# The last feature block of the down-projection, cut by token blocks at the kernel's end

## The chip, the cores and the metric

The kernel runs on one core of one Trainium2 chip. The metric is the device time of one execution in microseconds (us). The engines have short names: PE is TensorE (PEld its weight loads), DVE VectorE, ACT ScalarE, POOL GpSimd, and SP is SyncE, which here only issues DMAs.

## The reference, cut to what matters

One trunk layer of a streaming encoder over 1024 prompt tokens and 32 sample tokens. Only its end is touched by the change, the second half of the feed-forward block and the final norm:

```python
x = x + gt2 * ((jax.nn.silu(g) * up) @ w_down)      # D_FF = 2816 -> D_MODEL = 1024
y = x * rsqrt(mean(x * x, axis=-1) + EPS) * g_final # for prompt and sample
```

## The kernel before

**Layout.** Activations lie with the features on the 128 partitions and the tokens along the free dimension: `x2[j]` (j from 0 to 7) holds 128 of the 1024 residual features for all 1056 tokens. The tokens are worked on in three thirds of 352. The final norm sums over features, so at the end each 128 x 128 piece of `x2[j]` is transposed on PE; the output rows leave with tokens on the partitions.

**Down-projection of the last third.** The loop at the end of the listing (L2228) makes, for tokens `cut` = 704 to 1056 and for one feature block j after the other, a product over 22 K tiles (`NF`; the hidden features in blocks of 128). A float32 product is made of three single passes (`PASSES`: high x high, low x high, high x low, in fp32r), each with a weight load of 128 columns of its own: 66 matmuls of 352 columns for each j. They add up in one PSUM bank, `acc`. The weights of a feature block come in three parts of 8, 8 and 6 K tiles (`chunks`); DMA brings a part into `wraw`, ACT and DVE split it into high and low tiles (`wsp`, four of them, L417 and L418), and `W.use` / `W.used` keep the order of these steps. `piece_of[k, 2]` are the split activations of the K tile. After the 66 matmuls DVE adds `gt2 * acc` to `x2[j]` (L2249, 320 prompt and 32 sample columns).

**The end.** While the loop runs, the first 704 tokens are normalised and stored beside it (`finish_some`, `Finish`). For the last third there is the class `End`: three token blocks (`cuts`) of 128, 128 and 96 tokens (the last is 64 prompt and 32 sample tokens). After the first eight K tiles of j = 7, `ahead` transposes features 0 to 6 of all three blocks on PE, squares and sums them on ACT, adds the sums on POOL and multiplies the first 512 features by `g_final` (`gB`) on DVE; the remaining 14 K tiles of j = 7 (42 matmuls) run after its transposes. After DVE's add, `last` transposes the three pieces of j = 7, squares them, and makes 1/sqrt on POOL; then per block ACT scales features 0 to 511, DVE scales features 512 to 1023, and each half row is stored by its own DMA, one issued from ACT's queue and one from SP's.

**What sets the order.** Each engine runs its instructions in the order in which the code issues them; semaphores between the engines are placed by the framework, from which tile is written and read by whom.

Of the kernel before, what the change touches and what calls it, by code (L numbers as in the profile page):

```python
# [17 lines left out]
P = 128  # L18
# [36 lines left out]
class Weights:  # L55
# [8 lines left out]
    def add(self, block):  # L64
        self.blocks.append(block)
# [74 lines left out]
def hybrid_stream_step(  # L140
# [2024 lines left out]
    class End:  # L2165
# [9 lines left out]

        def take(self, j0, j1, part):
            for i, (a, b) in enumerate(self.cuts):
                h, n = j0 // 4, b - a
                py = self.py[i][h]
                for j in range(j0, j1):  # L2180
                    pe.transpose(py[:n, (j - 4 * h) * P:(j - 4 * h + 1) * P], x2[j][:, a:b], ident)
                act.activation(self.ys[i][:n, j0 * P:j1 * P], py[:n, (j0 - 4 * h) * P:(j1 - 4 * h) * P], AF.Square,
                               scale=D ** -0.5, accum_out=self.st[:n, part, i:i + 1])

        def ahead(self):
            self.take(0, 4, 0)
            self.take(4, KD - 1, 1)
            st = self.st
            pool.tensor_tensor(st[:, 0], st[:, 0], st[:, 1], op=ALU.add)
            pool.tensor_scalar(st[:, 0], st[:, 0], 1.0, EPS, op0=ALU.mult, op1=ALU.add)  # L2190
            for y, py, (a, b) in zip(self.ys, self.py, self.cuts):
                dve.tensor_tensor(y[:b - a, :512], py[0][:b - a], gB[:b - a, :512], op=ALU.mult)

        def last(self):
            self.take(KD - 1, KD, 2)
            st = self.st
            for i in range(3):
                pool.tensor_tensor(st[:, 0, i:i + 1], st[:, 0, i:i + 1], st[:, 2, i:i + 1], op=ALU.add)
                pool.tensor_tensor(st[:, 3, i:i + 1], st[:, 0, i:i + 1], mhalf[:, 0:1], op=ALU.pow)
            for i, (y, py, (a, b)) in enumerate(zip(self.ys, self.py, self.cuts)):  # L2200
                n, r = b - a, st[:b - a, 3, i:i + 1]
                act.activation(y[:n, :512], y[:n, :512], AF.Copy, scale=r)
                dve.scalar_tensor_tensor(y[:n, 512:], py[1][:n], r, gB[:n, 512:], op0=ALU.mult, op1=ALU.mult)
                for eng, cs in ((act, slice(0, 512)), (sp, slice(512, D))):
                    for q, u, v in col_segments(a, b):
                        out = y_sample[0, u - S:v - S] if q else y_prompt[0, u:v]
                        eng.dma_start(out[:, cs], y[u - a:v - a, cs])

# [19 lines left out]
    for j in range(KD):  # L2228
        if j == KD - 1:
            side.drain(job)  # L2230
            end = End()
        acc = bank()
        for w, (k0, k1) in zip(w_d1[j], chunks):
            wt = W.use(w)
            for k in range(k0, k1):
                while steps and (min(k + 4, NF - 1), 2) not in piece_of:
                    steps.pop(0)[2]()
                for q, (u, v) in enumerate(PASSES):
                    pe.matmul(acc, wt[(k - k0) // 4][:, u, (k - k0) % 4], piece_of[k, 2][:, v],  # L2239
                              start=(k == 0 and q == 0), stop=(k == NF - 1 and q == 2))  # L2240
                if k % 2 == 1:
                    side.tick()
            W.used(w)
            if j == KD - 1 and k0 == 0:
                end.ahead()
        while steps:
            steps.pop(0)[2]()
        for c, a, b in col_segments(cut, T):
            dve.scalar_tensor_tensor(x2[j][:, a:b], acc[:, a - cut:b - cut], gt2[:, c, j:j + 1], x2[j][:, a:b],  # L2249
                                     op0=ALU.mult, op1=ALU.add)  # L2250
    end.last()
    close_sl()
# [35 lines left out]
```

## Time and profile before

| what | us |
|---|---|
| median of 3 runs | 1606.16 |
| the runs | 1605.96 to 1606.76 |
| the profiled execution, its own time | 1606.87 |
| its span, first to last instruction | 1604.8 |
| PE's last matmul of the projection ends at | 1595.2 |

The profiled execution lies 0.7 us over the median, and 2.07 us of its time lie around the span. All times of the trace below count from the start of the span. How to read the page: busy shares are of the whole span; matmuls overlap, and the ends of their records are modelled, so the pace of a row of matmuls is its whole length divided by their number and not the duration of one.

### The profile page before, as it was taken

The page shows a single profiled execution, that of the slowest core. Times are in us where ns is not written, and L with a number is a line of the kernel's source. Part 1 is how long each engine was busy: PE and PEld are TensorE (multiplying, and loading weights), DVE is VectorE, ACT ScalarE, POOL GpSimd, SP SyncE. Part 2 cuts the span into 40 slices and gives each one's busy share as a digit, 9 for nine tenths or more (in the row PEclk, how much of TensorE's full clock was granted, in tenths as well). Part 3 has the DMA queues.
Part 4 walks back from the last instruction along what each step waited for, and adds up shares of the span by engine and source line. Part 5 has one row for each costly group of instructions (what it writes and reads, how often), then busy time and mean ns, then how long its engine had stood idle before and what let it go on. Part 6 is the DMA issues. An engine that isn't in the chain of part 4 may idle for free.

```text
span 1604.8 us, 27381 instructions
## 1 busy us (share of the span) xinstructions
PE 1575.5 (98%) x10244; PEld 1554.0 (97%) x10244; DVE 1138.7 (71%) x2186; ACT 785.9 (49%) x1747; POOL 446.0 (28%) x477
## 2 busy tenths in 40 slices
PE   7999999999999999999999999999999999999997
PEld 6989999999999999999999999999999999999997
DVE  7766564646776855546654699988898986799754
ACT  3655463544455644444443655554544444545443
POOL 2344243434332411000012100565565650000001
PEclk9999999999999999999999999999999999999999
DMA  9823323232222232675353311313222227427453
GB/s 361 276 72 92 98 82 102 88 122 84 70 80 80 67 96 70 121 268 176 121 152 114 106 54 46 102 54 106 81 80 94 67 82 253 135 79 250 133 157 126
DMA packets 210414, 192.45 MB, mean 120 GB/s; under 512 B 10706, under 2 KB 180618, under 8 KB 209258
## 3 DMA queue, kind: packets, MB, share of 16 engines
q1 hardware_dynamic: 205386, 187.82, 37.4%
q10 hardware_dynamic: 4640, 2.82, 0.6%
q8 instruction: 81, 1.33, 0.4%
q14 instruction: 51, 0.42, 0.1%
q0 software_dynamic: 256, 0.06, 0.0%
HBM read 152.19 MB, written 41.63 MB: 121 GB/s over the span
## 4 chain that ended last, share of the span: by engine, by line
PE 88%; DVE 5%; DMA 3%; ACT 2%; issue 1%; SPq 0%; ACTq 0%; POOL 0%; DVEq 0%; POOLq 0%
PE mm L451 39%; PE psb L1836 18%; PE mm L1836 10%; PE mm L2239 3%; PE mm L900 3%; PE psb L2239 2%; PE psV L799 2%; PE psb L2082 2%; PE psS L741 1%; DMA s<-in_w_ada_dram 1%; PE psT L768 1%; PE mm L2082 1%; DMA wraw<-in_w_in_dram 1%; DMA t<-in_x_sample_dram 1%; DVE st L755 1%
## 5 line engine op out<-in xcount | busy, mean ns | idle before, releaser
L451 PE MATMUL mm<-s,wsp 128*128 128x352 f32 x4104 | 689.1, 324 | 0.0
L451 PEld LDWEIGHTS mm<-s,wsp 128*128 128x128 f32 x4104 | 656.8, 188 | 2.0 <-issue 0.4
L418 DVE TENSOR_TENSOR wsp<-wraw,wsp 128x512 fp32r<-128x512 f32 (+1 forms) x280 | 236.6, 861 | 119.2 <-ACT wsp L417 117.6
L1836 PE MATMUL psb<-s,wsp 128*128 128x352 f32 x1611 | 271.7, 322 | 1.5 <-DVE wsp L418 0.8
L417 ACT ACTIVATE wsp<-wraw 128x512 fp32r<-128x512 f32 x336 | 199.6, 617 | 138.8 <-PE psb L1836 40.8
L1836 PEld LDWEIGHTS psb<-s,wsp 128*128 128x128 f32 x1611 | 260.5, 188 | 2.1 <-DVE wsp L418 1.1
L1836 PE MATMUL mm<-s,wsp 128*128 128x352 f32 x933 | 159.3, 322 | 0.0
L1836 PEld LDWEIGHTS mm<-s,wsp 128*128 128x128 f32 x933 | 151.2, 188 | 0.5 <-DVE wsp L418 0.5
L761 POOL TENSOR_SCALAR st<-st,mx 128x640 f32<-128x640 f32 (+5 forms) x72 | 56.6, 785 | 184.2 <-DVE mx L760 169.9
L1223 DVE SCALAR_TENSOR_TENSOR t<-wa,cmix,t 128x512 f32<-128x512 f32 x112 | 88.7, 797 | 15.2 <-DMA wa<-in_w_ada_dram 14.9
L418 POOL TENSOR_TENSOR wsp<-wraw,wsp 128x512 fp32r<-128x512 f32 x56 | 75.8, 1375 | 49.1 <-ACT wsp L417 47.5
L756 ACT ACTIVATE st<-st,mx 128x640 f32<-128x640 f32 (+5 forms) x72 | 47.9, 666 | 71.3 <-DVE mx L755 70.0
L755 DVE CUSTOM_DVE_ANT_0 st<-psS,bias 128x640 f32<-128x640 f32 (+5 forms) x72 | 44.3, 616 | 46.1 <-PE psS L741 33.6
L1783 POOL TENSOR_TENSOR t<-t,sl 128x352 f32<-128x352 f32 x19 | 18.3, 962 | 185.3 <-ACT sl L1781 185.3
L775 ACT ACTIVATE pT<-psT 128x640 fp32r<-128x640 f32 (+3 forms) x80 | 38.7, 494 | 62.9 <-PE psT L768 48.0
L2151 POOL TENSOR_TENSOR fst<-fst 128x1 f32<-128x1 f32 (+1 forms) x6 | 1.2, 194 | 236.6 <-ACT t L2144 236.6
L780 DVE TENSOR_TENSOR pT<-psT,pT 128x640 fp32r<-128x640 f32 (+3 forms) x80 | 44.0, 558 | 22.7 <-ACT pT L775 22.5
L1446 POOL TENSOR_TENSOR wraw<-wraw,raw 128x512 f32<-128x512 f32 x33 | 55.8, 1703 | 0.9
L900 PE MATMUL mm<-s,s 128*128 128x264 f32 (+3 forms) x432 | 54.8, 283 | 0.0
L2239 PE MATMUL mm<-s,wsp 128*128 128x352 f32 x330 | 54.4, 324 | 0.0
L2239 PEld LDWEIGHTS mm<-s,wsp 128*128 128x128 f32 x330 | 53.1, 188 | 0.0
L1446 POOL TENSOR_TENSOR wraw<-wraw 128x512 f32<-128x512 f32 x22 | 32.6, 1482 | 71.4 <-DVE wsp L418 70.6
(392 smaller groups left out, 2543.0 us busy)
## 6 DMA issues: line engine op xcount, KB each, us to landing
wraw<-in_w_in_dram SPq DMA_DIRECT2D x38, 512.0 KB, 3.9
wraw<-in_w_gate_up_dram SPq DMA_DIRECT2D x33, 512.0 KB, 3.7
wa<-in_w_ada_dram SPq DMA_DIRECT2D x64, 256.0 KB, 3.2
wraw<-in_w_down_dram SPq DMA_DIRECT2D x32, 512.0 KB, 3.7
a_d<-t SPq DMA_DIRECT2D x22, 528.0 KB, 2.7
g_d<-t SPq DMA_DIRECT2D x16, 528.0 KB, 5.1
x<-xres SPq DMA_DIRECT2D x16, 528.0 KB, 6.5
t<-g_d SPq DMA_DIRECT2D x16, 528.0 KB, 5.0
```

Source lines behind the costliest of these rows:

```text
L417: act.activation(dst[:, 0], src, AF.Copy)
L418: eng.tensor_tensor(dst[:, 1], src, f(dst[:, 0]), op=ALU.subtract)
L451: pe.matmul(pt[:, :hi - lo], wt[(w0 + k) // 4][:, a, (w0 + k) % 4], xt[k][:, b, lo:hi], start=(k == 0 and q == 0), stop=(k == n - 1 and q ...
L755: dve.tensor_tensor_reduce(so, sv, bi, -1.0, 3.0e38, ALU.add, ALU.min, mx[:n, 1:2])
L756: act.activation(st[:n, :w], st[:n, :w], AF.Exp, bias=mx[:n, 1:2], scale=-1.0, accum_out=mx[:n, 2:3])
L761: pool.tensor_scalar(st[:n, :w], st[:n, :w], mx[:n, 3:4], 1.0, op0=ALU.mult, op1=ALU.mult)
L900: pe.matmul(pt[:n, :wd], hs[k][:, a, i * P:i * P + n], whl[b][:, k, :wd], start=(k == 0 and q == 0), stop=(k == KD - 1 and q == 2))
L1223: dve.scalar_tensor_tensor(ac[:, c], wa, cmix[:, c, k:k + 1], ac[:, c], op0=ALU.mult, op1=ALU.add)
L1446: self.eng.tensor_tensor(a(dst), a(x), a(y), op=op)
L1836: pe.matmul(acc, wt[:, a, k], x[k][:, b], start=(start and not onto and k == 0 and q == 0), stop=(stop and k == 3 and q == 2), skip_group_ ...
L2082: pe.matmul(acc, wt[k // 4][:, u, k % 4], piece_of[k, i][:, v], start=(k == 0 and q == 0), stop=(k == KP - 1 and q == 2))
L2239: pe.matmul(acc, wt[(k - k0) // 4][:, u, (k - k0) % 4], piece_of[k, 2][:, v], start=(k == 0 and q == 0), stop=(k == NF - 1 and q == 2))
```

## The change

The last 14 K tiles of feature block 7 are no longer multiplied with all 352 tokens at once. They run three times, with tokens 704 to 832, 832 to 960 and 960 to 1056, over the same weight tiles, into the matching columns of `acc`. `End.last` is split: `norm` (transpose, square, POOL's 1/sqrt) and `put` (the scalings and the stores) work on one block. The norm of a block stands behind the products of the next block, `put` of the first block behind the add of the third. A block's two halves leave in one DMA of whole rows: from SP's queue for prompt rows, from ACT's for the 32 sample rows. Both weight parts are split before `ahead`, no longer one before and one behind it.

```diff
-        def last(self):
-            self.take(KD - 1, KD, 2)
+        def norm(self, i):
+
+            self.take(i, KD - 1, KD, 2)
             st = self.st
-            for i in range(3):
-                pool.tensor_tensor(st[:, 0, i:i + 1], st[:, 0, i:i + 1], st[:, 2, i:i + 1], op=ALU.add)
-                pool.tensor_tensor(st[:, 3, i:i + 1], st[:, 0, i:i + 1], mhalf[:, 0:1], op=ALU.pow)
-            for i, (y, py, (a, b)) in enumerate(zip(self.ys, self.py, self.cuts)):
-                n, r = b - a, st[:b - a, 3, i:i + 1]
-                act.activation(y[:n, :512], y[:n, :512], AF.Copy, scale=r)
-                dve.scalar_tensor_tensor(y[:n, 512:], py[1][:n], r, gB[:n, 512:], op0=ALU.mult, op1=ALU.mult)
-                for eng, cs in ((act, slice(0, 512)), (sp, slice(512, D))):
-                    for q, u, v in col_segments(a, b):
-                        out = y_sample[0, u - S:v - S] if q else y_prompt[0, u:v]
-                        eng.dma_start(out[:, cs], y[u - a:v - a, cs])
+            pool.tensor_tensor(st[:, 0, i:i + 1], st[:, 0, i:i + 1], st[:, 2, i:i + 1], op=ALU.add)
+            pool.tensor_tensor(st[:, 3, i:i + 1], st[:, 0, i:i + 1], mhalf[:, 0:1], op=ALU.pow)
+
+        def put(self, i):
+            (a, b), y = self.cuts[i], self.ys[i]
+            n, r = b - a, self.st[:b - a, 3, i:i + 1]
+            act.activation(y[:n, :512], y[:n, :512], AF.Copy, scale=r)
+            dve.scalar_tensor_tensor(y[:n, 512:], self.py[i][1][:n], r, gB[:n, 512:], op0=ALU.mult, op1=ALU.mult)
+            for q, u, v in col_segments(a, b):
+                out = y_sample[0, u - S:v - S] if q else y_prompt[0, u:v]
+                (act if q else sp).dma_start(out, y[u - a:v - a])
...
+        def products(wt, k0, k, a, b):
+            for q, (u, v) in enumerate(PASSES):
+                pe.matmul(acc[:, a - cut:b - cut], wt[(k - k0) // 4][:, u, (k - k0) % 4],
+                          piece_of[k, 2][:, v, a - cut:b - cut], start=(k == 0 and q == 0),
+                          stop=(k == NF - 1 and q == 2), skip_group_check=j == KD - 1)
...
         for w, (k0, k1) in zip(w_d1[j], chunks):
+            if j == KD - 1 and k0:
+                continue
...
+    wts = [(W.use(w), *c) for w, c in zip(w_d1[-1][1:], chunks[1:])]
+    end.ahead()
+    for i, (a, b) in enumerate(end.cuts):
+        for wt, k0, k1 in wts:
+            for k in range(k0, k1):
+                products(wt, k0, k, a, b)
+        if i:
+            end.norm(i - 1)
+        add(a, b)
+        if i == 2:
+            end.put(0)
+    end.norm(2)
+    end.put(1)
+    end.put(2)
```

On PE before, the last matmuls of the projection (`mm_16820` is `acc`, the last number of a row the columns) and behind them the three transposes of feature block 7; the rows name the semaphores that an instruction waits for:

```order
L2239 MATMUL mm_16820<-s_9586,wsp_16884 128x352
L2239 MATMUL mm_16820<-s_9630,wsp_16884 128x352 x3
L2181 MATMUL psb_16810<-ident,x_1827_14160 128x128 [waits DVE_49]
L2181 MATMUL psb_16812<-ident,x_1827_14160 128x128
L2181 MATMUL psb_16814<-ident,x_1827_14160 96x128 [waits DVE_49]
```

On PE in the change, the border between the second and the third token block:

```order
L2238 MATMUL mm_16820<-s_9586,wsp_16852 128x128 x3
L2238 MATMUL mm_16820<-s_9630,wsp_16852 128x128 x3
L2181 MATMUL psb_16810<-ident,x_1827_14160 128x128 [waits Activation_49]
L2238 MATMUL mm_16820<-s_10447,wsp_16821 128x96 [waits DVE_49]
L2238 MATMUL mm_16820<-s_10447,wsp_16821 128x96 x2
L2238 MATMUL mm_16820<-s_10291,wsp_16821 128x96 x3
```

The transpose of the first block stands between the blocks, and the first matmul of a new block carries a wait for DVE (the border between the first and the second block has it too, with no transpose ahead of it); its weights are those that the block before it has used already.

On DVE before, the end: the add of j = 7 and the three scalings of the second half rows (`t` is a row tile, `est` the 1/sqrt):

```order
L2249 SCALAR_TENSOR_TENSOR x_1827_14160<-mm_16820,amod_310,x_1827_14160 128x320 [waits PE_49]
L2249 SCALAR_TENSOR_TENSOR x_1827_14160<-mm_16820,amod_310,x_1827_14160 128x32
L2203 SCALAR_TENSOR_TENSOR t_16817<-psb_16810,est_16815,t_16006 128x512 [waits Activation_49,Pool_49]
L2203 SCALAR_TENSOR_TENSOR t_16818<-psb_16812,est_16815,t_16006 128x512 [waits Activation_49,Pool_49]
L2203 SCALAR_TENSOR_TENSOR t_16819<-psb_16814,est_16815,t_16006 96x512 [waits Activation_49,Pool_49]
```

On DVE in the change, the same place:

```order
L2244 SCALAR_TENSOR_TENSOR x_1827_14160<-mm_16820,amod_310,x_1827_14160 128x128 [waits PE_49] x2
L2244 SCALAR_TENSOR_TENSOR x_1827_14160<-mm_16820,amod_310,x_1827_14160 128x64 [waits PE_49]
L2244 SCALAR_TENSOR_TENSOR x_1827_14160<-mm_16820,amod_310,x_1827_14160 128x32
L2206 SCALAR_TENSOR_TENSOR t_16817<-psb_16810,est_16815,t_16006 128x512 [waits Activation_49,Pool_49]
L2206 SCALAR_TENSOR_TENSOR t_16818<-psb_16812,est_16815,t_16006 128x512 [waits Activation_49,Pool_49]
L2206 SCALAR_TENSOR_TENSOR t_16819<-psb_16814,est_16815,t_16006 96x512 [waits Activation_49,Pool_49]
```

The add is cut into one for each block, and all scalings, that of the first block too, stand behind the add of the third block.

## Rows read from the trace of the kernel before

**Rows 1.** The page: instructions, busy time and share; the chain that ended last.
```profile
PE 1575.5 (98%) x10244; PEld 1554.0 (97%) x10244; DVE 1138.7 (71%) x2186; ACT 785.9 (49%) x1747; POOL 446.0 (28%) x477
...
PE 88%; DVE 5%; DMA 3%; ACT 2%; issue 1%; SPq 0%; ACTq 0%; POOL 0%; DVEq 0%; POOLq 0%
```

**Rows 2.** Chain of waits, 1582 to 1605: start, length, what, count.
```profile
1588.37 6.79 PE mm L2239 x42
1595.17 0.02 issue
1595.19 0.56 DVE x L2249
1595.75 0.04 issue
1595.80 0.34 PE psb L2181
1596.14 0.02 issue
1596.16 0.38 ACT t L2182 x2
...
1597.53 0.73 ACT t L2202
```

**Rows 3.** Timeline, 1570 to 1606: start, length, engine, line, form, count.
```profile
1588.13 7.02 PE L2239 MATMUL mm<-s,wsp 128*128 128x352 f32 x42
...
1596.94 0.55 POOL L2199 TENSOR_TENSOR est<-est,mhalf 128x1 f32<-128x1 f32 x1
...
1597.53 2.32 DVE L2203 SCALAR_TENSOR_TENSOR t<-psb,est,t 128x512 f32<-128x512 f32 x3 [1.63 <-POOL est L2199]
...
1598.31 2.93 SPq L2207 DMA_DIRECT2D out_dram<-t  x4
...
1599.97 0.72 ACT L2202 ACTIVATE t<-t,est 96x512 f32<-96x512 f32 x1 [0.48 <-DVE t L2203]
1600.72 1.18 ACTq L2207 DMA_DIRECT2D out_dram<-t  x2
```

**Rows 4.** Timeline of weight loads, 24 to 38: each before one narrow matmul.
```profile
24.42 10.84 PEld L333 LDWEIGHTS psT<-csil,s 128*128 128x128 f32 x96
35.96 1.86 PEld L333 LDWEIGHTS psT<-csil,s 128*128 128x128 f32 x16 [0.69 <-DMA s<-in_w_ada_dram]
37.74 0.41 PEld L359 LDWEIGHTS psV<-ones,t 128*128 128x128 f32 x3
```

**Rows 5.** Timeline of PE, 88.9 to 89.4: two narrow fp32r matmuls of the attention scores.
```profile
88.73 0.48 PE L451 MATMUL mm<-s,wsp 128*128 128x352 f32 x2
89.05 0.33 PE L741 MATMUL psS<-s,s 128*128 128x128 f32 x2
89.22 0.38 PE L451 MATMUL mm<-s,wsp 128*128 128x352 f32 x1
```

**Rows 6.** Groups by shape, 1500 to the end: busy us, mean ns, idle before.
```profile
L2249 DVE SCALAR_TENSOR_TENSOR x<-mm,amod,x 128x320 f32<-128x320 f32 x5 | 2.8, 550 | 8.6 <-PE mm L2239 8.6
...
L2249 DVE SCALAR_TENSOR_TENSOR x<-mm,amod,x 128x32 f32<-128x32 f32 x5 | 1.2, 241 | 0.0
```

**Rows 7.** Who waited for whom, 1588 to the end: total us, times, longest.
```profile
PEld psb L2181 <- DVE x L2249: 0.9, 1, 0.9
PE psb L2181 <- DVE x L2249: 0.6, 1, 0.6
```

**Rows 8.** DMA, 1598 to 1604.8: GB/s in 40 slices of 0.17 us, packets.
```profile
GB/s 0 0 0 0 0 0 84 361 386 386 386 386 386 386 374 398 398 398 386 422 398 422 338 253 229 313 386 337 205 302 169 0 0 0 0 0 0 0 0 0
DMA packets 832, 1.44 MB, mean 212 GB/s; under 512 B 128, under 2 KB 128, under 8 KB 832
```

**Rows 9.** Stretches: engines' busy us (and instructions), PE's granted clock, DMA share, GB/s.
```profile
20.00:38.00 18.00, 17.07 (x148) 16.36 (x148) 16.69 (x15) 3.62 (x15) 3.05 (x2) 1.00 1.04 391
...
1588.00:1595.00 7.00, 7.00 (x46) 6.86 (x44) 2.23 (x5) 2.67 (x10) 0.39 (x2) 1.00 0.00 0
...
1595.00:1605.00 10.00, 0.70 (x4) 0.30 (x3) 2.95 (x5) 3.04 (x9) 2.16 (x6) 0.63 0.41 144
```

More of the change, by code (lines that the diff above doesn't have):

```diff
@@ L2174, in __init__, with take @@
             self.ys = [tmpt((P, D)) for _ in self.cuts]
[L2176 to L2183, printed above, removed]
+        def take(self, i, j0, j1, part):
+            a, b = self.cuts[i]
+            h, n = j0 // 4, b - a
+            py = self.py[i][h]
+            for j in range(j0, j1):
+                pe.transpose(py[:n, (j - 4 * h) * P:(j - 4 * h + 1) * P], x2[j][:, a:b], ident)
+            act.activation(self.ys[i][:n, j0 * P:j1 * P], py[:n, (j0 - 4 * h) * P:(j1 - 4 * h) * P], AF.Square,
+                           scale=D ** -0.5, accum_out=self.st[:n, part, i:i + 1])
         def ahead(self):
-            self.take(0, 4, 0)
-            self.take(4, KD - 1, 1)
+            for j0, j1, part in ((0, 4, 0), (4, KD - 1, 1)):
+                for i in range(3):
+                    self.take(i, j0, j1, part)
             st = self.st
@@ L2232, in hybrid_stream_step, with add @@
         acc = bank()
+        def products(wt, k0, k, a, b):
[3 more added lines that the diff above has]
+                          stop=(k == NF - 1 and q == 2), skip_group_check=j == KD - 1)
+        def add(a, b):
+            for c, a, b in col_segments(a, b):
+                dve.scalar_tensor_tensor(x2[j][:, a:b], acc[:, a - cut:b - cut], gt2[:, c, j:j + 1], x2[j][:, a:b],
+                                         op0=ALU.mult, op1=ALU.add)
         for w, (k0, k1) in zip(w_d1[j], chunks):
+            if j == KD - 1 and k0:
+                continue
             wt = W.use(w)
@@ L2237, in hybrid_stream_step @@
                     steps.pop(0)[2]()
-                for q, (u, v) in enumerate(PASSES):
-                    pe.matmul(acc, wt[(k - k0) // 4][:, u, (k - k0) % 4], piece_of[k, 2][:, v],
-                              start=(k == 0 and q == 0), stop=(k == NF - 1 and q == 2))
+                products(wt, k0, k, cut, T)
                 if k % 2 == 1:
@@ L2243, in hybrid_stream_step @@
             W.used(w)
-            if j == KD - 1 and k0 == 0:
-                end.ahead()
         while steps:
             steps.pop(0)[2]()
[L2248 to L2251, printed above, removed]
+        if j < KD - 1:
+            add(cut, T)
+    wts = [(W.use(w), *c) for w, c in zip(w_d1[-1][1:], chunks[1:])]
[12 more added lines that the diff above has]
+    end.put(2)
     close_sl()
```

## The prediction

> **What bounds the kernel now.** I read the page first. PE is busy 98% of the span and carries 88% of the chain that ended last; the weight loads fill 97% [rows 1]. So nearly everything is PE's pace, and a change of the end is worth what it does to PE's last work and to what follows it. The chain of waits shows the end in order of time [rows 2]: 42 matmuls of 352 columns take 6.79 us, 0.162 us each, and end at 1595.16 (the timeline has the same stretch from 1588.13, 7.02 us with the last one's modelled end [rows 3]). From there PE is done but for three transposes: DVE's add 0.56, the transposes 0.34, the squares 0.38, POOL's root, and at 1597.53 the scalings begin. The timeline carries it on [rows 3]: DVE scales three half rows in 2.32, ACT's third scaling runs from 1599.97 to 1600.69, and the last two stores are issued in the 1.18 after 1600.72, the second at about 1601.3. The DMA rates show traffic from about 1599.1 to 1603.3 [rows 8]; the span ends at 1604.8. The tail behind PE's last matmul is 9.64 us, 2.4 before the first scaling, 5.8 until the last byte, 1.5 to close. The question is how much of these 9.64 moves beside PE, and what PE pays for it.
>
> **Part 1: PE pays for cutting the tokens.** The 42 matmuls become 126, as each token block needs all 14 K tiles with 3 passes. The columns in sum stay 352, but each matmul loads its 128-column weight anew. What a narrow matmul costs is shown by other lines: 96 loads of 128 columns before matmuls of 128 columns (L333) take 10.84 us [rows 4]. Without the last load's own length (about 0.19, as three take 0.41) that is 10.65 / 95 = 0.112 us; the 16 in 1.86 give 0.111; three loads before matmuls of 64 columns (L359) give (0.41 - 0.19) / 2 = 0.11. The pace does not fall with the columns: the load sets it, and 96 columns will cost what 128 do. Those operands are plain fp32, the ones here fp32r. The nearest fp32r rows are the attention scores (L741): two matmuls of 128 columns and the start of the next lie within 89.22 - 89.05 = 0.17 us, 0.085 each [rows 5]; the load of the first lay ahead there, so this is an end of the range and not the pace of a stream. Nothing speaks for a slower rate for narrow fp32r. The other end is the 0.162 of today. I take 0.112, the only row from a long stream: 126 x 0.112 = 14.1, less 6.8, is **+7.3 us**; 0.085 would give +3.9, and 0.118 (a little lost at the borders of weight tiles) +8.1.
>
> A rule stands against this reading. The Trainium skill's page "TensorE: Matmul & The Clock Gate" (section "Back-to-back issue gap") gives about 81 ns as the sustained pace of a load and a matmul of 128 columns. Its table of weight modes says that the fast load is not for FP32. An estimate by the 81 ns is 126 x 0.081 - 6.8 = +3.4. The rows of L333 disagree with it here.
>
> **Part 2: PE waits twice for DVE.** In the order, the first matmul of the second and of the third block carries a wait for DVE. All blocks sum in one tile `acc`, and the only new DVE work that touches it is the add of the block before. So PE stops while DVE reads. Worked from the chain: PE's end to DVE 0.03, the add, DVE's end to PE 0.05, and 0.34 until the first restarted result, less the 0.11 that it takes in a stream [rows 2]. The add of 128 columns lies between 0.241 for 32 and 0.55 for 320 [rows 6]; on the line between them it is 0.34. One wait is 0.03 + 0.34 + 0.05 + 0.34 - 0.11 = 0.65, two are **+1.3 us**; the first block's transpose (0.11) lies inside the second. Ends: 0 if the wait is met in time, and 0.9 each as PE's loads waited for the 320-column add [rows 7]. Queued behind the waiting matmul is all of PE, so nothing hides this.
>
> **Part 3: what leaves the tail.** I count from PE's last projection matmul. The first block's squares and root are done long before: its transpose stands ahead of the third block's products. But its scaling does not run beside them: on DVE all three scalings stand behind the third add, which waits for PE's last matmul; on ACT the first scaling stands behind the second block's square, whose transpose stands behind PE's last matmul too. So the tail keeps all three scalings:
> - DVE: adds of 64 and 32 columns until 0.5, then block 1's half at 0.5 to 1.25.
> - PE transposes block 2 at once (0.11), ACT squares it at 0.15. From the first square to the use of the root takes 1597.53 - 1596.16 = 1.37 [rows 2], so block 2's factor is there at 1.5.
> - ACT: square to 0.5, block 1's scaling 0.73 to 1.26; store 1 goes out at 1.3. Block 3's transpose (add at 0.5, +0.34) is ready at 0.9, but its square waits for ACT until 1.27. Its factor is there at 1.27 + 1.37 = 2.64; POOL's two steps per block (0.55 the longer [rows 3]) keep up.
> - Block 2: ACT 1.6 to 2.4, DVE 1.5 to 2.3, store 2 at 2.4. Block 3: both from 2.64 to 3.4, stores at 3.4 from SP and ACT at once.
>
> Before, the last store was issued at 6.1. DMA gains less: the same 1.44 MB must leave at the 0.386 MB/us of most slices [rows 8], which is 1.36, 1.36 and 1.02 us for the three blocks. Traffic begins about 0.85 after an issue (1598.3 to 1599.1), so the blocks land at 2.15 + 1.36 = 3.5, 4.9 and 5.9, and with the 1.5 to close the tail is 7.4 instead of 9.64: **-2.3 us**. Ends: -3.0 if the last issue alone sets it (3.4 + 2.0 from issue to last byte as before + 1.5 = 6.9) and whole rows move a little faster; -1.5 if ACT's and POOL's steps queue worse than I count.
>
> **Part 4: at nothing.** The last weight part is split ahead of the squares: ACT does it while PE is at the first eight K tiles and the 21 transposes, and the first block needs it only after 24 matmuls, 2.7 us in. The squares and DVE's products with `g_final` slip by some 1 us; the first add stands behind them on DVE, but 4.7 us after the transposes. If that cover were gone, it would cost the 1 us. Fewer DMAs (4 instead of 8) save issue time that is in part 3. SP's queue holds nothing else.
>
> **Sum.** +7.3 + 1.3 - 2.3 = +6.3 us. The profiled execution would go from 1606.87 to 1613.2; the median of the runs lies 0.7 under it, so 1606.16 + 6.3 = **1612.5 us**, 0.39% slower.
>
> **The rivals.**
> 1. Not slower: weight loads hide and narrow matmuls cost by their columns. Then the 126 take the 6.8 us that the 42 take, and 1.3 - 2.3 = -1.0 gives 1605.2. For it: the 0.085 of rows 5. Against it: 112 loads of L333 that never went under 0.11, with matmuls of 64 columns no faster. It decides at a pace of 0.087: under that, the change is within 0.2% of before; at 0.062 it is even. The rule of 81 ns named above would come to an estimate of 3.4 + 1.3 - 2.3 = +2.4, 1608.6, on this side too. Chance 6%.
> 2. PE's clock falls. It was granted 1.00 of 2.4 GHz through the narrow stream (20 to 38) and the last matmuls; in the idle tail the mean is 0.63, so it fell towards 1.2 GHz after PE had stopped [rows 9]. Two pauses of 0.65 us and half-empty matmuls might bring that forward. Bound: if the pace doubled over all three blocks, +14.1, 1626.6; over the last alone +4.7, 1617.2. The Trainium skill tells on the same page (section "HAM oscillation") of a narrow kernel that lost its clock between bursts; no run here shows that yet, and the narrow stream of rows 9 speaks against it. Chance 4%.
> 3. No wait at the borders (PE finds the add done): 1611.2; inside the range.
> 4. The tail shrinks far more than I count. Parts 1 and 2 cost 8.6 of its 9.64 us, so it cannot make the change faster at their full price; with -5.5 instead of -2.3 the time would be 1609.3, just within 0.2%. Against it: all three scalings stay in the tail by the order of DVE and ACT. Chance 2%.
>
> **How the numbers follow.** Forecast 88% (with rival 3), rival 1 6%, rival 2 4%, rival 4 2%. The forecast's own ends: -0.4 to +0.8 on the pace, -1.3 to +0.5 on the waits, -0.7 to +0.8 on the tail; taken together unlikely, so 1610.0 to 1614.6. About 0.2%, 3.2 us, is what a measurement of this kernel can tell from no change: slower needs over 1609.4, faster under 1602.9. Slower 0.90; the same 0.08 (most of rival 1); faster 0.02.
>
> **What would show it.** In the changed kernel's timeline: 42 matmuls of 128 columns in about 4.7 us (6.8 before for the whole); PE idle some 0.4 to 0.7 us before the second and the third block, released by DVE's add; PE's last matmul 8.6 us later than before, at about 1603.8; the first store about 1.3 us after it, the last at 3.4; a tail of about 7.4. The prediction is wrong if 42 narrow matmuls take under 3.7 us, if the granted clock drops ahead of PE's end, or if the tail is under 6 us.

## The result and the profile after

The changed kernel takes 1614.15 us in the median of nine runs (1612.87 to 1618.72), beside 1606.65 for the kernel before on the same chip. The ratio is 1.0044, with a 95% interval from 1.0031 to 1.0057: slower by 0.44%. The forecast was 1612.5, with a range of 1610.0 to 1614.6. Four of the nine runs lie close together at 1612.87 to 1613.19, and the other five spread upwards from 1614.15. What parts the two groups is the subject of most of the experiments below.

The profiled execution took 1616.03 us, with a span of 1614.2. Its page answers to [rows 1]:

```profile
PE 1586.3 (98%) x10328; PEld 1564.1 (97%) x10328; DVE 1139.3 (71%) x2188; ACT 785.9 (49%) x1747; POOL 445.6 (28%) x477
...
PE 90%; DVE 4%; DMA 2%; ACT 2%; issue 1%; POOL 0%; SPq 0%; POOLq 0%; ACTq 0%; DVEq 0%
```

PE has 84 instructions more (126 matmuls instead of 42), is busy 10.8 us longer, and still carries the chain. The chain of waits has the stretch of [rows 2], start, length, what and count:

```profile
1588.22 4.66 PE mm L2238 x42
1592.88 0.02 issue
1592.90 0.36 DVE x L2244
1593.26 0.04 issue
1593.31 4.92 PE mm L2238 x42
1598.23 0.02 issue
1598.25 0.36 DVE x L2244
1598.61 0.04 issue
1598.66 7.66 PE mm L2238 x42
```

The three token blocks stand one behind the other, with DVE's add between them as the only link. The first two blocks took some 4.7 to 4.9 us each, as forecast. The third, which has fewer columns, took 7.66. The timeline shows the same with the waits (start, length, engine, line, form, count, idle time ahead and who ended it); it answers to [rows 3]:

```profile
1587.95 4.77 PEld L2238 LDWEIGHTS mm<-s,wsp 128*128 128x128 f32 x42
1587.98 4.88 PE L2238 MATMUL mm<-s,wsp 128*128 128x128 f32 x42
...
1593.31 4.91 PE L2238 MATMUL mm<-s,wsp 128*128 128x128 f32 x42 [0.45 <-DVE x L2244]
...
1598.66 7.66 PE L2238 MATMUL mm<-s,wsp 128*128 128x96 f32 x42 [0.31 <-DVE x L2244]
...
1607.61 2.44 SPq L2209 DMA_DIRECT2D out_dram<-t  x3
...
1607.91 1.61 DVE L2206 SCALAR_TENSOR_TENSOR t<-psb,est,t 128x512 f32<-128x512 f32 x2 [0.45 <-POOL est L2200]
...
1609.60 0.39 ACTq L2209 DMA_DIRECT2D out_dram<-t  x1
```

Why the third block took so long stands in the view by stretches (length, then busy time and instructions of PE, PEld, DVE, ACT, POOL, then PE's granted clock, DMA share, GB/s), as [rows 9]:

```profile
1588.00:1593.00 5.00, 4.86 (x45) 4.72 (x42) 1.15 (x3) 1.69 (x8) 0.38 (x2) 1.00 0.00 0
1593.30:1598.00 4.70, 4.70 (x42) 4.70 (x42) 0.00 (x0) 0.00 (x0) 0.00 (x0) 1.00 0.00 0
1598.60:1600.30 1.70, 1.64 (x15) 1.65 (x15) 0.00 (x1) 0.15 (x2) 0.74 (x2) 1.00 0.00 0
1600.40:1606.30 5.90, 5.90 (x30) 5.88 (x29) 0.00 (x0) 0.00 (x0) 0.00 (x0) 0.50 0.00 0
```

The clock was granted at 1.00 (2.4 GHz) through the first two blocks and for 1.7 us of the third, and at 0.50 (1.2 GHz) for the rest. Some 27 of the 42 matmuls then ran at about 0.21 us each instead of 0.112, and the block took 2.8 us more than the 4.9 of the block ahead of it. PE was busy without a gap in that stretch, so it waited for nothing: it was slow. PE's last matmul ends at 1606.32, 11.2 us later than before, where the forecast had 8.6; the slow stretch makes up the difference.

The DMA rates in 40 slices of 0.18 us from 1607 to 1614.2 answer to [rows 8]:

```profile
GB/s 0 0 0 0 0 0 0 0 432 410 410 387 432 410 387 387 478 387 410 432 432 341 319 159 273 68 273 432 387 341 23 0 0 0 0 0 0 0 0 0
```

The bytes of the stores leave from about 1608.4 to 1612.6, and there is a dip in the 24th to 26th slice. In it the store of the 32 sample rows moves, which leaves from ACT's queue: from 1611.1 to 1611.7 the trace has 0.09 MB of its 128 KB, in 23 packets that take 75% of the DMA engines' time. The last 0.26 MB from SP's queue come behind it. From PE's last matmul to the end of the span the tail is 7.9 us, where it was 9.64.

### The profile page after: what moved, and what is told of

It reads as the page before. It is cut to its first block, busy times and chain, and to the rows that moved or that the text cites. A ratio compares the mean times of both kernels' runs of the same rounds, so it can differ in the third digit from the quotient of the medians.

```text
span 1614.2 us, 27550 instructions
## 1 busy us (share of the span) xinstructions
PE 1586.3 (98%) x10328; PEld 1564.1 (97%) x10328; DVE 1139.3 (71%) x2188; ACT 785.9 (49%) x1747; POOL 445.6 (28%) x477
## 4 chain that ended last, share of the span: by engine, by line
PE 90%; DVE 4%; DMA 2%; ACT 2%; issue 1%; POOL 0%; SPq 0%; POOLq 0%; ACTq 0%; DVEq 0%
PE mm L451 40%; PE psb L1836 18%; PE mm L1836 10%; PE mm L2238 4%; PE mm L900 3%; PE psb L2238 2%; PE psV L799 2%; PE psb L2082 2%; PE psS L741 1%; PE psT L768 1%; DMA s<-in_w_ada_dram 1%; PE mm L2082 1%; DMA t<-in_x_sample_dram 1%; PE psV L1134 1%; PE mm L483 1%
## 5 line engine op out<-in xcount | busy, mean ns | idle before, releaser
L451 PE MATMUL mm<-s,wsp 128*128 128x352 f32 x4104 | 689.4, 324 | 0.0
L451 PEld LDWEIGHTS mm<-s,wsp 128*128 128x128 f32 x4104 | 656.8, 188 | 2.3 <-issue 0.4
L1836 PE MATMUL mm<-s,wsp 128*128 128x352 f32 x933 | 159.2, 322 | 0.0
L1836 PEld LDWEIGHTS mm<-s,wsp 128*128 128x128 f32 x933 | 151.2, 188 | 0.5 <-DVE wsp L418 0.3
L2238 PE MATMUL mm<-s,wsp 128*128 128x352 f32 (+2 forms) x414 | 64.8, 318 | 0.8 <-DVE x L2244 0.8
L2238 PEld LDWEIGHTS mm<-s,wsp 128*128 128x128 f32 x414 | 63.3, 198 | 1.1 <-DVE x L2244 1.1
L900 PEld LDWEIGHTS mm<-s,s 128*128 128x128 f32 (+1 forms) x432 | 51.9, 179 | 0.5
```

The lines of the kernel that those rows point to most:

```text
L451: pe.matmul(pt[:, :hi - lo], wt[(w0 + k) // 4][:, a, (w0 + k) % 4], xt[k][:, b, lo:hi], start=(k == 0 and q == 0), stop=(k == n - 1 and q ...
L900: pe.matmul(pt[:n, :wd], hs[k][:, a, i * P:i * P + n], whl[b][:, k, :wd], start=(k == 0 and q == 0), stop=(k == KD - 1 and q == 2))
L1836: pe.matmul(acc, wt[:, a, k], x[k][:, b], start=(start and not onto and k == 0 and q == 0), stop=(stop and k == 3 and q == 2), skip_group_ ...
L2238: pe.matmul(acc[:, a - cut:b - cut], wt[(k - k0) // 4][:, u, (k - k0) % 4], piece_of[k, 2][:, v, a - cut:b - cut], start=(k == 0 and q == ...
```

## The experiments

Two questions were open: whether the terms of the sum hold one by one, and what makes the clock fall in the third block. For the clock there were three theories. A: matmuls this narrow, 128 columns or 96, let it fall. B: the two pauses of PE between the blocks bring it about. C: it goes with the block of 96 columns alone. Where a ratio is given, it is to the kernel before, run on the same chip beside it.

### nopause: the same blocks without the waits

Each block adds up in another PSUM bank than the one that DVE reads, and the first eight K tiles are added ahead of them.

```diff
...
     end.ahead()
+    add(cut, T)
+    accs = [bank(), acc]
     for i, (a, b) in enumerate(end.cuts):
+        acc = accs[i % 2]
         for wt, k0, k1 in wts:
             for k in range(k0, k1):
-                products(wt, k0, k, a, b)
+                products(wt, k0, k, a, b, wts[0][1])
```

(The last argument is the K tile with which a sum begins.)

> The change with the first eight K tiles added to x2 early and the three token blocks summed in two PSUM banks by turns, so that PE need not wait for DVE at the borders of the blocks. Still 126 narrow matmuls. Both theories: the two pauses (0.5 to 0.6 us of PE idle each) are gone and 42 narrow matmuls take 4.7 us, so 1.2 us less than the changed kernel where its clock holds: about 1611.8. Theory A (matmuls that fill the array for half of their time let the granted clock fall): the clock still falls ahead of PE's end in part of the runs, which scatter upwards by 1 to 5 us as those of the changed kernel do. Theory B (PE's two pauses bring the fall): no run falls, and they lie within 1 us of each other.

Measured: 1612.2 us in the median of twelve runs (1611.37 to 1613.35), ratio 1.0025 [1.0011, 1.0038]. The timeline of PE:

```profile
1587.32 9.58 PE L2238 MATMUL mm<-s,wsp 128*128 128x128 f32 x84
1596.74 0.29 PE L2181 MATMUL psb<-ident,x 128*128 128x128 f32 x1
1596.79 5.52 PE L2238 MATMUL mm<-s,wsp 128*128 128x96 f32 x42
```

Blocks 1 and 2 are one stream, and no wait is left at a border. The lowest run is 1.5 us under the lowest of the changed kernel, which fits the price of the two waits (1.2 by the trace, below). The third block still takes 5.52 instead of 4.9: the clock fell in its last part here, as the stretches show:

```profile
1587.40:1596.70 9.30, 9.30 (x86) 9.30 (x85) 1.97 (x5) 1.63 (x8) 0.38 (x2) 1.00 0.00 0
1597.00:1601.40 4.40, 4.40 (x40) 4.40 (x39) 0.29 (x1) 0.37 (x2) 0.74 (x2) 0.93 0.00 0
1601.40:1602.20 0.80, 0.80 (x6) 0.80 (x5) 0.00 (x0) 0.00 (x0) 0.00 (x0) 0.50 0.00 0
```

So the pauses are not needed for the fall, and theory B loses its main support.

### widepause: the pauses without the narrow matmuls

The kernel before, with two copies of the accumulator by DVE into a scratch tile, for which PE waits.

```diff
...
                 if k % 2 == 1:
                     side.tick()
+                if j == KD - 1 and k in (12, 17):
+                    dve.tensor_copy(end.ys[0][:, 7 * P:], acc[:, :P])
```

> The kernel before, with the 42 wide matmuls stopped twice: after K tiles 12 and 17 DVE copies 128 columns of acc to a scratch tile and PE waits for that, as it waits for the adds in the change. Columns for each weight stay 352. Both: two pauses of about 0.6 us, so before plus 1.2, about 1607.9. Theory A (narrow matmuls let the clock fall): no fall before PE's end, the scatter is that of before (under 1.5 us). Theory B (the pauses do): in part of the runs the clock falls behind a pause, and they are 2 us and more above the others.

Measured: 1608.4 us (twelve runs, ten of them 1607.86 to 1609.47), ratio 1.0014 [1.0000, 1.0028]. The two pauses are there, in PE's timeline:

```profile
1587.33 2.68 PE L2239 MATMUL mm<-s,wsp 128*128 128x352 f32 x15
1590.88 2.66 PE L2239 MATMUL mm<-s,wsp 128*128 128x352 f32 x15 [0.87 <-DVE t L2245]
1593.92 2.19 PE L2239 MATMUL mm<-s,wsp 128*128 128x352 f32 x12 [0.38 <-DVE t L2245]
```

The three stretches keep their pace of before (15 in 2.68, against 42 in 7.02 in [rows 3]), so the clock held. Two pauses cost about 1.8 us here, and nothing else. The two other runs took 1616.06 and 1616.92, and theory B expected some runs 2 us and more above the rest. But they lie about 8 us over it, and a fall right behind the first pause would add only the 27 matmuls behind it once more, 4.4 us at 0.162 each. The kernel before has three such runs beside them (1614.1 to 1614.68). With nopause, B is refuted from both sides: a fall without pauses, and pauses without a fall.

### narrowlong: twice as many narrow matmuls

The changed kernel, with the last 14 K tiles of feature block 6 cut in the same way, without a wait between the pieces.

```diff
...
+            if j == KD - 2 and k0:
+                for a, b in ((cut, cut + P), (cut + P, cut + 2 * P), (cut + 2 * P, T)):
+                    for k in range(k0, k1):
+                        products(wt, k0, k, a, b)
...
```

> The change, and the last 14 K tiles of feature block 6 cut into the same three token blocks as well, without any wait there: 84 more matmuls in a stream that no wait interrupts. Both: 126 x 0.112 - 6.8 = 7.3 us more than the changed kernel while the clock holds, about 1620.4. Theory A (narrow matmuls let the clock fall): the fall can come in block 6 already, in more runs and earlier, so the median is 2 to 14 us above 1620.4. Theory B (the pauses do): the fall stays behind the pauses of feature block 7, median 1620.4 to 1622.

Measured: 1621.1 us in the median of four runs (1619.78 to 1622.6), ratio 1.0085 [1.0061, 1.0109]. PE's timeline, the added cut first, and then the three blocks of the change:

```profile
1574.24 14.25 PE L2238 MATMUL psb<-s,wsp 128*128 128x128 f32 x126
...
1594.47 4.88 PE L2238 MATMUL mm<-s,wsp 128*128 128x128 f32 x42
1599.80 4.91 PE L2238 MATMUL mm<-s,wsp 128*128 128x128 f32 x42 [0.44 <-DVE x L2244]
...
1605.15 4.89 PE L2238 MATMUL mm<-s,wsp 128*128 128x96 f32 x42 [0.31 <-DVE x L2244]
```

The 126 matmuls take 14.25 us where the 42 wide ones take 7.02: the forecast's +7.3 for a cut, seen a second time. The clock was 1.00 all through them (42 of them have 96 columns), which speaks against theory A. The median is also what theory B expected; what speaks against B is nopause and widepause. In this execution the clock held to the end of the last block too and fell right behind it (0.52 from 1609.9 to 1610.3), and in that block 42 matmuls of 96 columns take the 4.9 us of 42 of 128. So the load sets the pace at either width, and the long third block of the other profile is the clock alone.

### mid96 and mid128: the width alone, away from the end

Both are the kernel before with feature block 6's last 14 K tiles cut into four pieces. PE is in the midst of its work there, waits for no add, and feature block 7 and the end are untouched. The two kernels differ in the pieces' width alone; mid128's pieces overlap, and the columns that two of them share are added twice. mid96:

```diff
+            if j == KD - 2 and k0:
+                for a, b in ((0, 96), (96, 192), (192, 288), (288, T - cut)):
+                    for k in range(k0, k1):
+                        for q, (u, v) in enumerate(PASSES):
+                            pe.matmul(acc[:, a:b], wt[(k - k0) // 4][:, u, (k - k0) % 4], piece_of[k, 2][:, v, a:b],
+                                      start=False, stop=(k == NF - 1 and q == 2), skip_group_check=True)
...
```

> The kernel before, but the last fourteen K tiles of feature block 6 (one block ahead of the end, in the midst of PE's stream) are multiplied in pieces of 96, 96, 96 and 64 tokens, with no wait for DVE in between; feature block 7 and the end are those of before. The 42 matmuls become 168: at 0.112 us each 18.8 instead of 6.8, +12.0, so 1618.4 if the clock holds, with runs that agree within 1 us. Theory C (streams of 96 columns or fewer let PE's clock fall, those of 128 do not): the granted clock falls to 0.5 within this stretch, the pace goes from 0.112 to 0.21 for what is left of it, so 1621 to 1634, with runs several us apart. Rival D (the fall belongs to the end of the kernel, to the waits or to the engines going idle there, not to the width): the clock stays at 1.00 in the stretch, 1618.4.

mid128:

```diff
-                for a, b in ((0, 96), (96, 192), (192, 288), (288, T - cut)):
+                for a, b in ((0, 128), (96, 224), (192, 320), (224, T - cut)):
```

> mid96 with one size changed: its 168 narrow matmuls stand at the same place and load the same weights, but each multiplies 128 columns instead of 96 or 64 (pieces of tokens 0 to 128, 96 to 224, 192 to 320 and 224 to 352, so some columns of the third are added twice and this part of the sum is not the reference's). In mid96 the clock fell 5.2 us into the stretch and the 168 took 31.35 us. Theory C (the width decides): the clock stays at 1.00, 168 x 0.112 = 18.8 us, so 1618.4, within 1 us from run to run. Rival (any long narrow stream loses the clock, or a quirk of the place): it falls within the stretch as in mid96, 1625 to 1634.

Measured: mid96 1632.9 us (five runs, four of them 1631.24 to 1632.92), ratio 1.0165 [1.0141, 1.0188]. mid128 1619.16 us (six runs, four of them 1618.17 to 1619.38), ratio 1.0073 [1.0046, 1.0101]. They ran on two chips, on which the kernel before has medians of 1606.38 and 1607.41. The profiled executions of both are among the longer ones: they lose some 8 us in the first 50 us of the span, far from the edit, so the stretch itself is what is compared. The loss begins at one wait of PE for POOL, here in the kernel before and then in mid96 (mid128 has the same 6.88):

```profile
23.24 1.26 PE L257 MATMUL mm<-ident,rstd 128*128 128x128 f32 x9 [0.42 <-POOL rstd L310]
...
29.70 2.21 PE L257 MATMUL mm<-ident,rstd 128*128 128x128 f32 x9 [6.88 <-POOL rstd L310]
```

The granted clock behind it is 0.75 in the mean from 30 to 40 us. That the runs some 8 us over the rest in other kernels have this wait too is likely, but no profile shows it. PE's timeline of mid96, then of mid128:

```profile
1582.82 31.35 PE L2239 MATMUL psb<-s,wsp 128*128 128x96 f32 x168
1613.99 6.22 PE L2249 MATMUL mm<-s,wsp 128*128 128x352 f32 x24
```

```profile
1582.53 18.96 PE L2239 MATMUL psb<-s,wsp 128*128 128x128 f32 x168
1601.32 4.09 PE L2249 MATMUL mm<-s,wsp 128*128 128x352 f32 x24
```

The same 168 matmuls over the same weights take 12.4 us longer with fewer columns, and the wide stream behind them loses another 2.1. By stretches, mid96 and then mid128:

```profile
1582.80:1587.00 4.20, 4.20 (x41) 4.20 (x38) 1.03 (x2) 2.00 (x6) 1.46 (x4) 1.00 0.68 223
1587.00:1588.00 1.00, 1.00 (x12) 1.00 (x11) 0.00 (x0) 0.00 (x0) 0.00 (x0) 0.98 0.83 241
1588.00:1589.00 1.00, 1.00 (x7) 1.00 (x7) 0.00 (x0) 0.00 (x0) 0.00 (x0) 0.50 0.26 77
...
1590.00:1600.00 10.00, 10.00 (x49) 10.00 (x48) 1.18 (x2) 1.26 (x2) 0.00 (x0) 0.50 0.01 2
```

```profile
1582.80:1588.00 5.20, 5.20 (x49) 5.20 (x49) 1.03 (x2) 1.71 (x6) 1.46 (x4) 1.00 0.68 224
1588.00:1595.00 7.00, 7.00 (x65) 7.00 (x64) 1.55 (x3) 1.26 (x2) 0.00 (x0) 1.00 0.02 5
1595.00:1602.00 7.00, 7.00 (x63) 7.00 (x62) 1.62 (x4) 1.11 (x2) 0.00 (x0) 1.00 0.17 37
```

In mid96 the clock goes from 1.00 to 0.50 within the second piece of 96 columns and stays there, with PE busy all the time (10.00 of 10.00 us). It came back within the wide matmuls that followed (0.66 from 1618 to 1619, then 1.00). In mid128 it is 1.00 from the first matmul to the last. The lowest run of mid96 lies 3.2 us over the highest of mid128, so this is no accident of one execution. The mean granted clock over the span, which every run has, says the same: 0.987 to 0.990 in all five of mid96, 0.996 to 0.998 in all six of mid128. Theory C holds here: the stream of 96 columns lost the clock, and the same stream with 128 columns kept it. Theory A is out, and rival D of the expectation (the fall belongs to the kernel's end) with it.

### pad128, pad128b, nopauseb and first96: the width at the end

pad128 is nopause with a third block of 128 columns; the 32 further columns are multiplied and thrown away. pad128b and nopauseb are further runs of pad128 and nopause, beside each other.

```diff
...
-                products(wt, k0, k, a, b, wts[0][1])
+                products(wt, k0, k, b - P if i == 2 else a, b, wts[0][1])
```

> The kernel without pauses (own PSUM banks for the blocks), with the third token block's matmuls widened from 96 to 128 columns: the 32 columns more are products of the second block's tokens, go to unused PSUM columns and are thrown away. A narrow matmul costs 0.112 us either way, so PE's time is the same. Theory C (streams of 128 columns keep the clock, as 14.25 us of them in feature block 6 did; the block of 96 columns lets it fall): no run falls ahead of PE's end, all lie within about 1 us, median 1611.4 to 1611.8. Theory A (any narrow matmul): the scatter of nopause (1611.4 to 1613.4) stays.

> The same kernel as pad128 once more, for more runs beside nopause on the same chip: no waits at the borders, the third block with 128 columns of which 32 are thrown away. Theory C: nearly all runs at 1611.5 to 1611.9, none spread over 2 us. Rival (any narrow stream loses the clock now and then): a scatter like that of nopause, 1611.4 to 1613.4.

> The same kernel as nopause once more, beside pad128b: third block with 96 columns. Runs spread from 1611.4 to 1613.4 as the first time, as the clock falls in the third block at one time or another.

Measured: pad128 1611.8 us (five runs, three of them 1611.56 to 1611.8, the others 1613.0 and 1616.87), ratio 1.0040 [1.0028, 1.0052]; pad128b 1612.08 (twelve runs, 1611.61 to 1613.58), 1.0027 [1.0016, 1.0039]; nopauseb 1612.8 (eleven runs, 1611.53 to 1620.44), 1.0036 [1.0022, 1.0049]. PE's third block in the profile of pad128, and by stretches:

```profile
1596.75 4.89 PE L2238 MATMUL mm<-s,wsp 128*128 128x128 f32 x42
```

```profile
1597.00:1601.40 4.40, 4.40 (x42) 4.40 (x41) 0.25 (x1) 0.37 (x2) 0.74 (x2) 1.00 0.00 0
```

The block runs at full clock in both profiles of this kernel, and with a third more columns it is shorter than that of nopause (4.89 against 5.52). The transposes right behind PE's last block part the profiles in the same way: in the five kernels that end with 96 columns (the changed kernel, nopause, nopauseb, earlyput and narrowlong) the clock is at 0.50 to 0.52 in them, in the three that end with 128 (pad128, pad128b and first96) at 1.00. But the medians of the two kernels lie only 0.4 to 0.7 us apart, and pad128b has a scatter of 2 us of its own: three of its twelve runs lie at 1611.5 to 1611.9, where I expected nearly all. Some of the scatter is not the clock: pad128's 1616.87 has the mean clock of its shortest run, 0.998. So at the kernel's end the width explains the profiles, and not the whole scatter of the runs.

first96 is nopause with the narrower block first (96, 128 and 128 tokens).

```diff
...
-            self.cuts = [(a, min(a + P, T)) for a in range(cut, T, P)]
+            self.cuts = [(cut, cut + 96), (cut + 96, cut + 224), (cut + 224, T)]
```

> The kernel without pauses, with the token blocks cut as 96, 128, 128 in place of 128, 128, 96: the same 126 matmuls, the thinnest ones first. Theory C (the block of 96 columns lets the clock fall): in part of the runs the clock falls in the first block or soon behind it, and what follows goes at half the pace until the clock is granted again: up to 8 us above 1611.6, many runs over 1613.5. Rival (what lets it fall sits at the end, whatever the columns): the scatter of nopause, 1611.4 to 1613.4.

Measured: 1614.02 us (six runs: 1613.09 to 1614.04, and 1621.01 and 1622.83), ratio 1.0061 [1.0043, 1.0080]. In the profile, the 1613.09, the clock held to PE's end, through the 96 columns too. The 1622.83 has a mean clock of 0.991, where the short runs have 0.998 and no run of any other kernel but mid96 is under 0.995. As an estimate, 0.007 of 1621 us is 23 us at 0.50, which fits a fall in the first block that lasts through the other two. The 1621.01 (0.996, 8 us over the profiled run) fits the early loss of mid128's long runs as well. No profile shows either. Inconclusive.

### earlyput: the first block's scalings and store beside the third block

```diff
                 products(wt, k0, k, a, b)
+        if i == 2:
+            end.put(0)
         if i:
             end.norm(i - 1)
         add(a, b)
-        if i == 2:
-            end.put(0)
```

> The change, with the scalings and the store of the first token block issued ahead of the second block's last transpose and of the third add. The prediction said that the tail keeps all three scalings because of that order. If so, the first store goes out during the third block, ACT and DVE have two scalings left, and the tail behind PE's last matmul goes from 7.9 to about 7.0 us. Rival: the stores' bytes and the close set the tail, and it stays within 0.3 us of 7.9.

Measured: 1613.53 us (nine runs, 1612.85 to 1616.88), ratio 1.0042 [1.0030, 1.0054]. The timeline of the end:

```profile
1598.24 5.10 PE L2238 MATMUL mm<-s,wsp 128*128 128x96 f32 x42 [0.31 <-DVE x L2244]
...
1599.33 0.75 DVE L2206 SCALAR_TENSOR_TENSOR t<-psb,est,t 128x512 f32<-128x512 f32 x1 [1.15 <-POOL est L2200]
1600.15 6.85 SPq L2209 DMA_DIRECT2D out_dram<-t  x3
...
1606.55 0.39 ACTq L2209 DMA_DIRECT2D out_dram<-t  x1
```

The first store leaves at 1600.15, 3.2 us ahead of PE's end (1603.34). The span ends at 1611.06, a tail of 7.7 us instead of 7.9: taking a third of the bytes out of it gave 0.2 us. The last store is issued 3.2 us after PE's end, where it was 3.3, and the end moves with it. The 7.0 that I expected was wrong, and the rival came.

### widewhole: the rest of the change without the narrow matmuls

The 14 K tiles are multiplied with all 352 tokens, as before the change; the blocks' adds, norms, scalings and stores of whole rows stay.

```diff
+    for wt, k0, k1 in wts:
+        for k in range(k0, k1):
+            products(wt, k0, k, cut, T)
     for i, (a, b) in enumerate(end.cuts):
...
         add(a, b)
+        end.norm(i)
+    for i in range(3):
+        end.put(i)
```

> The change without its cut of the products: the last 42 matmuls with 352 columns as before, and the rest of the change kept (an add, a norm and a scaling for each token block, stores of whole rows). The prediction's part 3 without its parts 1 and 2. PE ends where it ended before. The first add of 128 columns lets the first transpose go 0.2 us earlier, the last store goes out at about 4.4 us behind PE's last matmul in place of 6.1, and the bytes end about 0.5 us earlier: 0.3 to 0.8 us under before. Rival: a store lands 2 to 3 us after its issue and the last one still sets the end as before: within 0.2 us of before.

Measured: 1606.16 us (twelve runs, all but one 1605.57 to 1607.02), ratio 1.0002 [0.9993, 1.0010], beside 1606.41. The timeline, and the DMA rates in 40 slices of 0.18 us from 1597 to 1604.3:

```profile
1597.69 2.03 SPq L2209 DMA_DIRECT2D out_dram<-t  x3
...
1599.27 0.39 ACTq L2209 DMA_DIRECT2D out_dram<-t  x1
```

```profile
GB/s 0 0 0 0 0 0 0 0 314 382 404 382 449 404 426 404 404 404 471 382 426 337 359 157 247 90 314 337 427 337 45 0 0 0 0 0 0 0 0 0
```

The last store goes out 4.6 us after PE's end (1594.63) instead of 6.1, and the time does not move: the 0.3 to 0.8 us that I expected are not there. What did not move is the first store: 3.06 us after PE's end, 3.15 before (1598.31 [rows 3] less 1595.16). From the first store's issue to the end of the span it is 6.6 us here, 6.5 in the kernel before (1598.31 to 1604.8) and 6.6 in the changed kernel (1607.61 to 1614.2). So in these three kernels the tail is the first store's issue and the 1.44 MB behind it, and when the later ones are issued does not matter. What the change costs thus comes from the narrow matmuls, their waits and their clock, and what it gains goes with the earlier first store.

### pair: a smaller price

Wide products up to K tile 12; the last ten K tiles for 224 and then for 128 tokens, in banks of their own, so that 60 matmuls replace 30.

```diff
+    for wt, k0, k in late[:LATER - 8]:
+        products(wt, k0, k, cut, T)
+    late = late[LATER - 8:]
...
+    for wt, k0, k in late:
+        products(wt, k0, k, cut, mid)
+    add(cut, T)
+    acc = bank()
+    for n, (wt, k0, k) in enumerate(late):
+        if n == 4:
+            end.norm(0)
+            end.norm(1)
             end.put(0)
+        products(wt, k0, k, mid, T, LATER)
+    add(mid, T)
```

> Another cut: wide matmuls up to K tile 12, then the last ten K tiles for 224 tokens and for 128 tokens, each sum in a bank of its own, the first 224 tokens (two blocks of 112) finished beside the products of the last 128. PE: 30 matmuls of 224 columns at 0.112 to 0.119 and 30 of 128 at 0.112 in place of 30 of 352 at 0.161, +2.1 us with the two transposes. Tail behind PE about 6.5 to 7 in place of 9.6, as only one block is left to scale and half of the bytes have gone. Together 0.5 to 1.0 us under before. Rival: the last stores still take 6 us from PE's end to the last byte, as in the kernel with the early first store, and the cut costs 0 to 1 us.

Measured: 1607.58 us (eleven runs, 1606.94 to 1612.1), ratio 1.0010 [1.0001, 1.0018]. It loses about 1 us, where I expected to gain 0.5 to 1.0. PE ends at 1597.05, 1.9 us later than before, and the first store leaves just behind it, at 1597.21; but the others leave at 1599.05 and 1600.16, and the span ends at 1605.85. As in earlyput, a first store that comes early enough leaves the end to the later ones. No version beat the kernel before.

## Why the prediction was right, and where it was not

**Part 1, the pace: right.** The 42 loads of the first block take 4.77 us; without the last one's own 0.19 that is 4.58 / 41 = 0.112 each, the number read from the long stream of [rows 4]. The two ends of the range, 0.085 and 0.118, were not needed; the range itself took only 0.4 us downwards on the pace, for which no row was given. That 96 columns cost what 128 do is shown by narrowlong's last block (4.89 and 4.91), at full clock. Rival 1 (a price by the columns) is out. The Trainium skill's page "TensorE: Matmul & The Clock Gate" (section "Back-to-back issue gap") gives about 81 ns for a load and a matmul of 128 columns; the trace disagrees, with 112 ns for these fp32r operands.

**Part 2, the waits: right, a little too large.** From the first matmul of one block to that of the next it is 5.33 us (1587.98 to 1593.31) and 5.35. Less 42 x 0.112 = 4.70, and less the transpose's 0.11 in the second, that is 0.63 and 0.54, in sum 1.2 where the forecast had 1.3. The view of waits names the releaser that the order showed:

```profile
PEld mm L2238 <- DVE x L2244: 1.1, 2, 0.6
PE mm L2238 <- DVE x L2244: 0.8, 2, 0.4
```

Rival 3 (no wait at the borders) is out; nopause, where the wait's cause is taken away, puts its price at 1.5 by the lowest runs.

**Part 3, the tail: the steps right, the sum too hopeful.** The first store came 1.3 us after PE's end, the second 2.4 and the last ones 3.3, as worked out (1.3, 2.4, 3.4). The last byte came at 6.3 instead of 5.9, and the close took 1.6. So the tail lost 1.75 us and not 2.3. The mis-sized term is the transfer: I took the 1.44 MB at the rate of most slices, with no dip between the stores, but in [rows 8] too the last third of the traffic has a dip, which I did not count. In the changed kernel it is the store of the sample rows, a step that I priced by its bytes alone. The kernel before gave the better price directly: 6.5 us from the first store's issue to the end, which with 1.3 makes 7.8.

**Part 4, nothing: right.** ACT's split of the last weight part (0.42 us, at 1585.96) lies beside PE's transposes, and PE does not wait for it.

**The sum.** With these sizes it is 7.3 + 1.2 - 1.75 = +6.75. The runs in which the four close times lie are 6.2 to 6.5 over the 1606.65 of before on the same chip, where I had forecast +6.3. The median of all nine, +7.5, lies in the forecast range as well, but that is luck: the sum has no term for the clock, and the profiled execution, in which the fall cost 2.8 us, lies over the range (1616.03 against 1614.6).

**Rival 2, the clock: thought unlikely, and it came.** In the profiled execution the clock fell 1.7 us into the last block. I had bounded that case at 1617.2 for the whole last block at half pace; it was 1616.03. A granted clock that drops ahead of PE's end was one of the signs of being wrong that the prediction named, and it came. I gave it 4 in 100, and of nine runs five lie over the close group. One of them, 1618.72, lies over the 1617.2 too, so the last block alone does not explain it. The step that failed is the reason against it: I read the narrow stream of [rows 9] as showing that narrow matmuls keep the clock. They do at the width that it shows, 128 columns, as narrowlong and mid128 confirm; it said nothing of 96. With [rows 4] the pace is the same for narrower matmuls, and I let one row stand for all widths for the clock too, where mid96 shows that this does not hold. Of the two reasons that the prediction named for a fall, the pauses were not it (nopause, widepause), and the half-empty matmuls went with one at 96 columns in some streams and at 128 in no profile.

The same page of the Trainium skill (section "HAM oscillation — how this bites in real kernels") tells of a kernel that lost its clock in waits for DMA between its bursts. mid96 shows another case: the clock stays at 0.50 in a stretch in which PE is busy 10.00 of 10.00 us.

**What stays open.** Of the changed kernel's runs only the profiled one shows where the clock fell. Of the others there is the mean over the whole span, 0.997 in the four close runs and 0.996 in the longer ones, where most runs of the kernel before near its median have 0.998 or 0.999. That the longer ones have their fall in the third block as well is argued, not shown, and the close four need not be free of one. Why it came early in that block here, late in nopause and earlyput and only behind it in narrowlong is open (the last two have the two pauses, so these do not decide it), and so is the scatter of 2 us that pad128b has with the full width.

## What to carry to other kernels

Cutting a matmul's columns costs a weight load for each piece that is added, and narrow pieces go at the pace of their loads (here 0.112 us for 96 as for 128 columns, against 0.162 for 352): three pieces doubled the time of the stretch. To bring stores forward, read from the trace what the tail hangs on, here the first store's issue and all the bytes after it; widewhole, which brought only the later stores forward, gained nothing. A row that shows the clock at 1.00 for one shape speaks for that shape only, and one execution does not settle it: the same 42 matmuls of 96 columns kept the clock to their end in narrowlong and lost it after 1.7 us in the changed kernel. Put the very shape into the midst of a stream, where PE's time stands apart from the end, and look at the granted clock.

## What the runs showed of the hardware

- A gap-free stream of fp32r matmuls with 96 columns (the last 42 of 168 with 64) and a load each began at a granted clock of 1.00 (2.4 GHz) and ran most of its length at 0.50 (1.2 GHz), 0.21 us each. The same stream with 128 columns kept 1.00 to its end. Multiplying more columns made the stretch 12.4 us shorter (18.96 against 31.35).
- A DMA of 512 KB that is alone begins to move bytes about 0.85 us after its issue. Of the two last stores of the changed kernel, both issued at 1609.6, the one of 128 KB from ACT's queue moves in a dip of the rate from 1611.1 to 1611.7 (0.09 MB at 75% of the DMA engines' time), and the one of 256 KB from SP's queue has its bytes behind it.
- A PE write into columns of a PSUM tile other than those that DVE was reading waited all the same for that read, as the framework's semaphores have it, and cost 0.54 to 0.63 us.
